# Expert slots of 64, 192, 128 and five of 64 rows, weight pieces split by 2048 columns, and a join by an identity product

## The chip, the cores and the metric

The kernel runs on one core of one Trainium2 chip, as one launch. The metric is device microseconds of that launch. Engines are named as the profile names them: PE (matrix products), DVE (vector), ACT (activation), POOL, and SP, whose queue issues the weight transfers.

## The reference

Two transformer-like blocks run one after the other on 256 tokens of width 1024. The first has two layers (attention with convolution, then a recurrent mixer) with two feed-forward nets each; the second has a mixer and a dense feed-forward net, then a mixer and a mixture of eight experts. The change is about the last stage, the experts, whose weights are some 277 MB of float32:

```python
def _moe(h, w_router, w_gate, w_up, w_down):
    logits = (h @ w_router).astype(jnp.float32)
    top_val, top_idx = lax.top_k(logits, TOP_K)          # TOP_K = 2
    top_w = jax.nn.softmax(top_val, axis=-1)
    gates = jnp.sum(jax.nn.one_hot(top_idx, N_EXPERTS, dtype=jnp.float32) * top_w[..., None], axis=-2)
    out = jnp.zeros_like(h)
    for e in range(N_EXPERTS):
        out = out + gates[..., e:e + 1] * _swiglu_2(h, w_gate[e], w_up[e], w_down[e])
    return out
# _swiglu_2(h, g, u, d) = (silu(h @ g) * (h @ u)) @ d;  h is 256 x 1024, g and u 1024 x 2816, d 2816 x 1024
```

With the reference's own inputs the router gives the eight experts 60, 49, 129, 90, 47, 57, 26 and 54 tokens.

## The kernel before

**Pieces and splits.** Every weight matrix is read in pieces of 1 MB (128 partitions x 2048 columns of float32) into a pool of four buffers, `raw`, by DMAs that SP issues (`load`, L300). An expert has 33 pieces: per chunk of 512 of the 2816 inner columns two for gate, two for up and two for down (the sixth chunk has 256 columns and half as many). `split` turns a piece into a high part and a low part, which PE takes in its fast float32 format: ACT copies with rounding (`wh`, recorded on the helper's line L222) and DVE subtracts the copy from the piece (`wl`, L231). It does so in halves of 1024 columns, each half in one of eight buffers of `wh` and of `wl`; in some of the earlier nets one or two further slots are added (`ext`). A raw buffer is free, and SP issues the next piece into it, when DVE has read it.

**Slots.** The tokens of an expert are gathered into a slot of fixed size. Expert 0 has slot 0; the others are put by size into slots 1 to 7. A slot of 128 rows has its tokens split in two operands, high and low, and takes three products per weight row of 128 (high with high, low with high, high with low; `mm3`, L334 to L337). A slot of 64 rows ("half") puts high and low side by side into one operand of 128 columns and takes two (`prod`, L429): rows 0 to 63 of the result hold the high part and rows 64 to 127 the low part, and these have to be added. Before, slots 0, 2, 3 and 4 hold 128 rows, slots 5, 6 and 7 hold 64, and slot 1, the largest expert, holds 128 + 64 rows ("big"), of which the second part works as a half. A count that doesn't fit is caught by a flag at the end, which runs all experts again in a loop for the rest.

**Order.** The slots run one after the other as `order = [0, 5, 2, 6, 3, 7, 4]`; the six chunks of the big slot are hung into them by the table `plan` (which run of the order and after which chunk). While one slot runs, the tables, gathered operands and gates of the next one are made in between (`tick`, `make`). The first chunk of expert 0 is computed for all 256 tokens ahead of the routing, and its rows are gathered afterwards (`head`). A scheduler then sets the order of all instructions on each engine from this program and the buffers.

**Joining.** For a half, `glu` joins high and low rows of the gate and of the up result: ACT copies rows 64 to 127 out of PSUM, DVE adds them to rows 0 to 63, ACT takes the Silu from SBUF, and DVE multiplies. `glu_T` then turns the result by PE transposes and splits it again for the down product. For a full slot ACT takes the Silu straight from PSUM and DVE multiplies with the other bank.

Of the kernel before, what the change touches and what calls it, by code (L numbers as in the profile page):

```python
# [8 lines left out]
F32 = mybir.dt.float32  # L9
# [183 lines left out]
class K:  # L193
    def __init__(self, ctx, tc, A, out, dbg=None):
# [3 lines left out]
        self.h_p = e(tc.tile_pool(name="wh", bufs=8))  # L198
        self.l_p = e(tc.tile_pool(name="wl", bufs=8))
# [106 lines left out]
    def split(self, raw, nk, n, pin=False):  # L306

        out = []
        per = max(1, 1024 // n)
        for k0 in range(0, nk, per):  # L310
            m = min(per, nk - k0) * n
            if self.ext and self.turn >= 8:
                hl = self.slot(self.ext[self.turn - 8], [128, 2, 1024], F32R)
                h, l = hl[:, 0], hl[:, 1]
            else:
                h = self.h_p.tile([128, 1024], F32R, tag="wh", name="wh")
                l = self.l_p.tile([128, 1024], F32R, tag="wl", name="wl")
            self.turn = (self.turn + 1) % (8 + len(self.ext))
            r = raw[:, k0 * n:k0 * n + m]
# [6 lines left out]
            out.append([(h[:, i * n:(i + 1) * n], l[:, i * n:(i + 1) * n]) for i in range(m // n)])  # L326
# [1067 lines left out]
    def moe(self, h, res, xT, defer):  # L1394
# [3 lines left out]
        lg = self.lg  # L1398

# [96 lines left out]
        def make(got, i, m, half, pcol, gcol):  # L1496
# [5 lines left out]
            eT = self.slot(i % 2, [128, 8, 128] if half else [128, 2, 8, 128], F32R)  # L1502
# [7 lines left out]
        first = make(got, 0, mt[:, 0:512], False, [pos[:, t, 0:1] for t in range(2)], None)  # L1510
# [45 lines left out]
        self.tt(over, cs[:, 0:1], cs[:, 2:3], OP.max)  # L1556
        self.stt(over, cs[:, 1:2], -64.0, over, OP.add, OP.max)
        self.stt(over, cs[:, 5:6], 64.0, over, OP.add, OP.max)
# [7 lines left out]
        self.ts(room, place, 1.0, 2.0, OP.is_equal, OP.add)  # L1566
        self.ts(place, place, 4.5, op0=OP.is_gt)
        self.tt(place, room, place, OP.subtract)
# [14 lines left out]
        def expert(src, got, out, **kw):  # L1583
# [7 lines left out]

            self.ffn(src, 0, got["xk"], [0], fin, half=got["half"], **kw)
# [279 lines left out]
```

## Time and profile before

| | |
|---|---|
| time, 3 runs | median 2261.82 us (2258.93 to 2261.97) |
| the profiled execution's own time | 2259.85 us |
| its span, first to last instruction | 2258.0 us |
| mean granted TensorE clock | 0.996 |
| busy, whole span | PE 97%, PE weight load 80%, DVE 76%, ACT 59%, POOL 4% |
| weight DMAs of the experts | 264 of 1 MB |

The shares are over the whole span, in which the stages differ. From about 1440 us on the experts run, and the table says little of them: the prediction reads that stretch by itself. PE's busy time counts matmuls whose ends overlap, so 97% does not mean that PE could do no more.

### The profile page before, as it was taken

What the parts mean: (1) busy time and instruction counts of PE and PEld (TensorE: products, weight loads), DVE (VectorE), ACT (ScalarE), POOL (GpSimd) and SP (SyncE); (2) the same over time, 40 slices, a digit from 0 to 9 for tenths busy, and PEclk for the clock granted to TensorE, in tenths of its full rate; (3) what the DMA queues carried; (4) which work ended last, traced back from release to release, by engine and by line L of the source; (5) the groups of instructions that cost most, each with busy time, mean ns of one, the idle gap of its engine ahead of it and who ended that gap; (6) DMA issues with size and microseconds to landing.
All of it is one profiled execution on the core that took longest, in us unless ns stands there. A gap on an engine that the chain in (4) does not pass through costs nothing.

```text
span 2258.0 us, 29602 instructions
## 1 busy us (share of the span) xinstructions
PE 2200.2 (97%) x10976; PEld 1812.7 (80%) x10976; DVE 1719.0 (76%) x2205; ACT 1336.0 (59%) x1819; POOL 92.9 (4%) x152
## 2 busy tenths in 40 slices
PE   8999999999999999999999999999999999999998
PEld 6888878888888788887888878887788777877777
DVE  6785967658657886675755666889888999889997
ACT  6445554445436744456544475677767776767764
POOL 0001000000000100030000111000000000000000
PEclk9999999999999999999999999999999999999999
DMA  8784258758764587533555442689988888989886
GB/s 339 267 317 163 99 191 318 258 194 311 262 222 159 193 318 264 207 130 131 215 186 183 143 160 108 249 338 336 336 331 326 326 335 320 344 329 347 325 328 242
DMA packets 82263, 572.92 MB, mean 254 GB/s; under 512 B 9373, under 2 KB 9685, under 8 KB 15424
## 3 DMA queue, kind: packets, MB, share of 16 engines
q1 hardware_dynamic: 77616, 556.73, 66.5%
q0 software_dynamic: 3920, 13.12, 1.7%
q8 instruction: 88, 1.44, 0.2%
q10 hardware_dynamic: 576, 1.11, 0.1%
q14 instruction: 63, 0.52, 0.1%
HBM read 569.80 MB, written 1.12 MB: 253 GB/s over the span
## 4 chain that ended last, share of the span: by engine, by line
PE 46%; DVE 5%; ACT 3%; issue 2%; DMA 1%; POOL 1%; ACTq 0%; DVEq 0%; POOLq 0%
PE mm L334 7%; PE mm L335 7%; PE mm L337 7%; PE mm L429 5%; PE acc L335 4%; PE acc L334 4%; PE acc L337 4%; DVE wl L231 3%; PE acc L429 2%; ACT wh L222 2%; PE mm L1579 1%; ACT s L222 1%; DVE s L231 1%; PE mm L595 1%; PE mm L1467 1%
## 5 line engine op out<-in xcount | busy, mean ns | idle before, releaser
L231 DVE TENSOR_TENSOR wl<-raw,wh 128x1024 fp32r<-128x1024 f32 (+1 forms) x908 | 1078.5, 1216 | 272.4 <-ACT wh L222 259.4
L222 ACT ACTIVATE wh<-raw 128x1024 fp32r<-128x1024 f32 (+1 forms) x908 | 921.0, 1052 | 371.4 <-PE mm L335 152.7
L334 PE MATMUL mm<-wh,s 128*128 128x512 f32 (+2 forms) x1384 | 515.9, 378 | 3.2 <-ACT s L222 3.2
L335 PE MATMUL mm<-wh,s 128*128 128x512 f32 (+2 forms) x1384 | 511.1, 374 | 1.0 <-DVE s L231 1.0
L222 ACT ACTIVATE s<-mm 128x512 fp32r<-128x512 f32 (+7 forms) x387 | 200.1, 534 | 346.8 <-PE mm L337 88.3
L337 PE MATMUL mm<-wl,s 128*128 128x512 f32 (+2 forms) x1384 | 396.1, 374 | 0.2
L334 PE MATMUL acc<-wh,s 128*128 128x512 f32 x788 | 312.0, 397 | 4.0 <-ACT s L222 2.1
L335 PE MATMUL acc<-wh,s 128*128 128x512 f32 x788 | 310.5, 394 | 2.2 <-DVE s L231 2.2
L334 PEld LDWEIGHTS mm<-wh,s 128*128 128x128 f32 x1384 | 261.2, 189 | 50.6 <-ACT s L222 4.9
L335 PEld LDWEIGHTS mm<-wh,s 128*128 128x128 f32 x1384 | 261.7, 189 | 47.7 <-DVE s L231 3.3
L337 PEld LDWEIGHTS mm<-wl,s 128*128 128x128 f32 x1384 | 249.5, 189 | 46.4 <-DVE wl L231 1.2
L337 PE MATMUL acc<-wl,s 128*128 128x512 f32 x788 | 251.9, 392 | 0.6 <-DVE wl L231 0.5
L334 PEld LDWEIGHTS acc<-wh,s 128*128 128x128 f32 x788 | 148.6, 189 | 35.5 <-ACT s L222 3.2
L335 PEld LDWEIGHTS acc<-wh,s 128*128 128x128 f32 x788 | 149.0, 189 | 32.4 <-DVE s L231 4.0
L337 PEld LDWEIGHTS acc<-wl,s 128*128 128x128 f32 x788 | 148.1, 189 | 32.5 <-DVE wl L231 2.2
L429 PE MATMUL mm<-wl,s 128*128 128x512 f32 (+1 forms) x384 | 144.1, 382 | 3.2 <-DVE wl L231 3.1
L429 PE MATMUL mm<-wh,s 128*128 128x512 f32 (+1 forms) x384 | 143.3, 381 | 0.0
L231 DVE TENSOR_TENSOR s<-mm,s 128x512 fp32r<-128x512 f32 (+5 forms) x216 | 128.7, 619 | 17.5 <-ACT s L222 16.7
L987 DVE SCALAR_TENSOR_TENSOR raw<-raw,s 128x1024 f32<-128x1024 f32 x96 | 114.2, 1219 | 4.5 <-DMA raw<-in_ada_w 2.6
L231 DVE TENSOR_TENSOR s<-s,mm 128x512 f32<-128x512 f32 (+1 forms) x93 | 59.6, 641 | 46.7 <-PE mm L337 41.1
L222 ACT ACTIVATE s<-raw 128x1024 fp32r<-128x1024 f32 x50 | 52.5, 1061 | 70.8 <-PE mm L337 33.0
L429 PEld LDWEIGHTS mm<-wl,s 128*128 128x128 f32 x384 | 72.5, 189 | 22.5 <-DVE wl L231 9.2
(308 smaller groups left out, 2187.5 us busy)
## 6 DMA issues: line engine op xcount, KB each, us to landing
raw<-in_moe SPq DMA_DIRECT2D x264, 1024.0 KB, 5.6
raw<-in_f SPq DMA_DIRECT2D x132, 1024.0 KB, 5.9
raw<-in_ada_w SPq DMA_DIRECT2D x48, 1024.0 KB, 5.0
raw<-in_dense SPq DMA_DIRECT2D x33, 1024.0 KB, 4.8
raw<-in_w_in SPq DMA_DIRECT2D x12, 1024.0 KB, 4.9
raw<-in_ow_in SPq DMA_DIRECT2D x8, 1024.0 KB, 5.0
raw<-in_w_out SPq DMA_DIRECT2D x8, 1024.0 KB, 6.2
raw<-in_ew_in SPq DMA_DIRECT2D x7, 1024.0 KB, 5.0
```

What stands on the lines that cost most here:

```text
L222: return self.nc.scalar.activation(out=out, in_=in_, func=func, **kw)
L231: return self.nc.vector.tensor_tensor(out=out, in0=in0, in1=in1, op=op)
L334: mm(out=out, lhsT=xs[i][0], rhs=ws[i][0], start=first and i == 0, stop=False)
L335: mm(out=out, lhsT=xs[i][1], rhs=ws[i][0], start=False, stop=False)
L337: mm(out=out, lhsT=xs[i][0], rhs=ws[i][1], start=False, stop=last and i == n - 1)
L429: self.nc.tensor.matmul(out=out, lhsT=x[0], rhs=w[j][:, c0:c0 + n], start=first and k == 0 and j == 0, stop=last and k == len(ws) - 1 and ...
L595: mm(out=out, lhsT=a, rhs=b, start=j == 0, stop=j == len(todo) - 1)
L987: self.nc.vector.scalar_tensor_tensor(out=src, in0=src, scalar=1.0, in1=self.c_row, op0=OP.mult, op1=OP.mult, accum_out=p[:, 2 * pc + i:2 ...
L1467: mm(out=p[:, k * w:(k + 1) * w], lhsT=h[t][:, a, kk * 128:(kk + 1) * 128], rhs=one[:, o:o + w], start=t == 0, stop=t == 1)
L1579: mm(out=p, lhsT=o[:, t * 128:(t + 1) * 128], rhs=v[:, sl], start=b == 0, stop=b == len(parts) - 1)
```

## The change

It has three parts, all felt mostly in the expert stage.

- **Slots.** Slots 0, 3 and 4 become halves too: the sizes are now 64, 192, 128, 64, 64, 64, 64, 64. The order is `[0, 3, 2, 4, 5, 6, 7]`, and the six chunks of the big slot are hung into runs 1, 3, 4, 4, 5 and 6. The flag's limits follow the sizes. By the counts above every expert fits (60 in slot 0; 129, 90, 57, 54, 49, 47, 26 in slots 1 to 7), so the loop behind the flag does not run.
- **Splits.** The buffers of `wh` and `wl` are four of 2048 columns instead of eight of 1024; two `ext` slots together make a fifth pair, and a single one is no longer used. In the expert stage a piece is copied and subtracted by one instruction each over 2048 columns; elsewhere still by halves of 1024, but both halves share one pair, which is free when both have been used.
- **Join.** For a half, ACT copies rows 64 to 127 of a bank to SBUF as before, but PE adds them to rows 0 to 63 by a product with a 64 x 64 identity that accumulates into the same bank (`self.eye`, `self.low`; the copy goes to the second half of the slot's operand tile). Silu and the multiplication then read PSUM. DVE's two additions are gone.

```diff
-        self.h_p = e(tc.tile_pool(name="wh", bufs=8))
-        self.l_p = e(tc.tile_pool(name="wl", bufs=8))
+        self.h_p = e(tc.tile_pool(name="wh", bufs=4))
+        self.l_p = e(tc.tile_pool(name="wl", bufs=4))
...
     def split(self, raw, nk, n, pin=False):
         out = []
-        per = max(1, 1024 // n)
+        if self.turn < 4:
+            pair = self.h_p.tile([128, 2048], F32R, tag="wh", name="wh"), self.l_p.tile([128, 2048], F32R, tag="wl", name="wl")
+        else:
+            pair = [self.slot(i, [128, 2048], F32R) for i in self.ext]
+        self.turn = (self.turn + 1) % (5 if len(self.ext) == 2 else 4)
+        hi, lo = pair
+        per = nk if self.in_moe else max(1, 1024 // n)
         for k0 in range(0, nk, per):
...
-                self.act(h[:, :m], r, AF.Copy)
+                self.act(hi[:, sl], raw[:, sl], AF.Copy)
...
-            ins = self.tt(l[:, :m], r, h[:, :m].bitcast(F32), OP.subtract)
+            ins = self.tt(lo[:, sl], raw[:, sl], hi[:, sl].bitcast(F32), OP.subtract)
...
     def glu(self, banks, n, g, u, half=False):
         if half:
-            g, u = g[0:64], u[0:64]
-            for v, p in ((g, banks[0]), (u, banks[1])):
+            for j, p in enumerate(banks):
+                v = self.low[0:64, j * 512:j * 512 + n]
                 self.act(v, p[64:128, :n], AF.Copy)
-                self.tt(v, p[0:64, :n], v, OP.add)
-            self.act(g, g, AF.Silu)
-            self.tt(u, u, g, OP.mult)
+                self.nc.tensor.matmul(out=p[0:64, :n], lhsT=self.eye[0:64, 0:64], rhs=v, start=False, stop=True,
+                                      skip_group_check=True)
+            self.act(g[0:64], banks[0][0:64, :n], AF.Silu)
+            self.tt(u[0:64], banks[1][0:64, :n], g[0:64], OP.mult)
             return
...
-        order = [0, 5, 2, 6, 3, 7, 4]
+        order = [0, 3, 2, 4, 5, 6, 7]
 
-        plan = {(6, 1): [(big_end, ())]}
-        for c, (i, at) in enumerate([(1, 4), (3, 0), (3, 3), (5, 0), (5, 3), (2, 2)]):
+        plan = {(6, 2): [(big_end, ())]}
+        for c, (i, at) in enumerate([(1, 4), (3, 1), (4, 0), (4, 4), (5, 3), (6, 0)]):
```

What this moves on the engines is shown at two places. The first is DVE in a run of a half slot beside the full slot's preparation: `wl<-raw,wh` is the split of a piece, `64x512` are the joins and multiplications of the half's chunk, `128x4x64` is the split of its turned result, and `CAST` belongs to the gathering of the next slot. Before (run 1, slot 5):

```order
L231 TENSOR_TENSOR s_227_11373<-mm,s_227_11373 64x512
L231 TENSOR_TENSOR wl<-raw,wh 128x1024 x2
L231 TENSOR_TENSOR s_227_11373<-mm,s_227_11373 64x512
L231 TENSOR_TENSOR wl<-raw,wh 128x1024
L231 TENSOR_TENSOR s_227_11373<-s_227_11373 64x512
L231 TENSOR_TENSOR wl<-raw,wh 128x1024
L231 TENSOR_TENSOR s_232_11634<-mm,s_232_11634 128x4x64
L231 TENSOR_TENSOR wl<-raw,wh 128x1024 x6
```

The same place of the change (run 1, slot 3):

```order
L231 TENSOR_TENSOR wl<-raw,wh 128x2048 x5
L231 TENSOR_TENSOR s_213_10981<-mm,s_213_10981 64x512
L231 TENSOR_TENSOR wl<-raw,wh 128x2048
L231 TENSOR_TENSOR s_218_11244<-mm,s_218_11244 128x4x64
L231 TENSOR_TENSOR wl<-raw,wh 128x2048 x2
L231 TENSOR_TENSOR s_213_10981<-mm,s_213_10981 64x512
```

Per chunk DVE has one instruction of `64x512` instead of three, and one long split per piece instead of two.

The second place is PE at the end of a half's up product (`mm<-wh` and `mm<-wl`), where the down product of the chunk before (`acc`) follows. Before (run 1) the one follows straight on the other:

```order
L429 MATMUL mm<-wh,s_235_11854 128x512
L429 MATMUL mm<-wl,s_235_11854 128x512
L429 MATMUL acc<-wh,s_232_11634 128x512
L429 MATMUL acc<-wl,s_232_11634 128x512
L429 MATMUL acc<-wh,s_232_11634 128x512
```

In the change (run 1) the identity product (L437) that joins the up bank stands one matmul behind the bank's last product:

```order
L428 MATMUL mm<-wh,s_221_11404 128x512
L428 MATMUL mm<-wl,s_221_11404 128x512
L428 MATMUL acc<-wh,s_218_11244 128x512
L437 MATMUL mm<-s_221_11404,rtr 64x512
L428 MATMUL acc<-wl,s_218_11244 128x512
```

PE now has, between the up product and the down product, an instruction that waits for ACT's copy, and the rest of the down product is queued behind it.

## Rows read from the trace of the kernel before

**Rows 1.** The page: busy us and share; tenths busy in 40 slices.

```profile
PE 2200.2 (97%) x10976; PEld 1812.7 (80%) x10976; DVE 1719.0 (76%) x2205; ACT 1336.0 (59%) x1819; POOL 92.9 (4%) x152
...
DVE  6785967658657886675755666889888999889997
...
DMA  8784258758764587533555442689988888989886
```

**Rows 2.** Windows of the expert stage: from:to us, length, busy of each engine, clock, DMA.

```profile
1440.00:2258.00 818.00, 790.86 (x3737) 629.92 (x3735) 730.75 (x778) 588.43 (x694) 0.00 (x0) 0.99 0.87 326
...
1528.00:1646.00 118.00, 113.88 (x542) 88.06 (x540) 109.43 (x121) 95.55 (x119) 0.00 (x0) 0.99 0.91 333
...
1901.00:2002.00 101.00, 99.83 (x484) 82.07 (x483) 85.78 (x85) 70.14 (x81) 0.00 (x0) 1.00 0.90 340
2002.00:2145.00 143.00, 135.12 (x609) 103.27 (x608) 135.00 (x152) 106.45 (x129) 0.00 (x0) 1.00 0.88 330
```

**Rows 3.** Waits of the SP queue, 1450 to 2250 us: total, times, longest.

```profile
SPq L300 <- DVE wl L231: 573.7, 223, 7.1
```

**Rows 4.** Tile raw, 1450 to 2250: duration ns min/median/max, first and last start; landing.

```profile
L231 DVE TENSOR_TENSOR wl<-raw,wh x506: 1202/1218/1227, 1449.2 to 2245.0; 128x1024 fp32r<-128x1024 f32 x169
L222 ACT ACTIVATE wh<-raw x504: 1037/1050/1068, 1449.2 to 2243.3; 128x1024 fp32r<-128x1024 f32 x168
L300 SPq DMA_DIRECT2D raw<-in_moe x249: 327/333/357, 1451.6 to 2233.1; - x125
...
DMA to landing us min/median/max: 4.7/5.7/8.8
```

**Rows 5.** Waits of DVE and ACT, 1450 to 2250 us: total, times, longest.

```profile
DVE wl L231 <- ACT wh L222: 44.3, 61, 2.7
...
ACT wh L222 <- DMA raw<-in_moe: 29.5, 35, 2.0
...
ACT wh L222 <- PE mm L335: 12.6, 27, 2.1
```

**Rows 6.** DVE groups by shape, 1440 to 2258 us: count, busy us, mean ns.

```profile
L231 DVE TENSOR_TENSOR wl<-raw,wh 128x1024 fp32r<-128x1024 f32 x512 | 602.4, 1217 | 49.8 <-ACT wh L222 46.1 <-PE acc L429 0.6
...
L231 DVE TENSOR_TENSOR s<-mm,s 64x512 f32<-64x512 f32 x40 | 27.0, 675 | 2.7 <-ACT s L222 2.7
...
L231 DVE TENSOR_TENSOR s<-s,mm 128x512 f32<-128x512 f32 x24 | 16.5, 686 | 10.5 <-PE mm L337 10.4
L231 DVE TENSOR_TENSOR s<-mm,s 128x512 fp32r<-128x512 f32 x24 | 16.4, 684 | 3.4 <-ACT s L222 3.3
...
L231 DVE TENSOR_TENSOR s<-s 64x512 f32<-64x512 f32 x20 | 13.5, 676 | 0.2
...
L231 DVE TENSOR_TENSOR s<-mm,s 128x256 fp32r<-128x256 f32 x25 | 10.3, 414 | 2.5 <-ACT s L222 2.4
...
L231 DVE TENSOR_TENSOR s<-mm,s 64x256 f32<-64x256 f32 x8 | 3.3, 411 | 0.9 <-ACT s L222 0.9
```

**Rows 7.** ACT groups by shape, 1440 to 2258 us.

```profile
L222 ACT ACTIVATE wh<-raw 128x1024 fp32r<-128x1024 f32 x511 | 509.5, 1051 | 67.0 <-DMA raw<-in_moe 29.5 <-PE mm L335 13.4 <-PE acc L335 9.0
...
L222 ACT ACTIVATE s<-mm 64x512 f32<-64x512 f32 x40 | 23.8, 595 | 31.2 <-PE mm L429 30.7
...
L222 ACT ACTIVATE s<-s 64x512 f32<-64x512 f32 x20 | 12.4, 621 | 1.8 <-DVE s L231 1.8
```

**Rows 8.** Timeline of PE inside a full slot: start us, us.

```profile
1712.28 0.39 PE L334 MATMUL mm<-wh,s 128*128 128x512 f32 x1
...
1713.19 0.39 PE L334 MATMUL mm<-wh,s 128*128 128x512 f32 x1
```

**Rows 9.** Windows with the highest DMA rates, and one with a lower clock.

```profile
15.00:20.00 5.00, 4.90 (x21) 3.73 (x20) 5.00 (x6) 4.67 (x6) 0.00 (x0) 1.00 1.02 412
...
1590.00:1600.00 10.00, 9.52 (x47) 7.10 (x46) 8.59 (x13) 8.05 (x11) 0.00 (x0) 1.00 1.01 404
...
1620.00:1630.00 10.00, 8.36 (x46) 6.85 (x45) 8.94 (x12) 6.84 (x11) 0.00 (x0) 0.83 0.78 265
```

**Rows 10.** Waits of ACT ahead of the experts, 0 to 1430 us.

```profile
ACT wh L222 <- PE mm L335: 138.2, 150, 3.2
```

More of the change, by code (lines that the diff above doesn't have):

```diff
@@ L308, in split @@
         out = []
-        per = max(1, 1024 // n)
-        for k0 in range(0, nk, per):
[L311 to L319, printed above, removed]
+        if self.turn < 4:
[5 more added lines that the diff above has]
+        per = nk if self.in_moe else max(1, 1024 // n)
+        for k0 in range(0, nk, per):
+            m = min(per, nk - k0)
+            sl = slice(k0 * n, (k0 + m) * n)
             with self.tc.issue_after(self.behind.ins) if self.behind else ExitStack():
-                self.act(h[:, :m], r, AF.Copy)
+                self.act(hi[:, sl], raw[:, sl], AF.Copy)
             self.behind = None
-            ins = self.tt(l[:, :m], r, h[:, :m].bitcast(F32), OP.subtract)
+            ins = self.tt(lo[:, sl], raw[:, sl], hi[:, sl].bitcast(F32), OP.subtract)
             if pin:
                 self.pin(ins)
-            out.append([(h[:, i * n:(i + 1) * n], l[:, i * n:(i + 1) * n]) for i in range(m // n)])
+            out.append([tuple(v[:, k * n:(k + 1) * n] for v in pair) for k in range(k0, k0 + m)])
         return out
@@ L1398, in moe @@
         lg = self.lg
+        self.eye = self.small("rtr", 128, F32R, bufs=1)
+        nc.vector.tensor_copy(out=self.eye, in_=self.ident)
         up0 = [self.piece(A["moe"][0], j * 128 * 2048, 4, 512) for j in range(4)]
@@ L1501, in make @@
             yield
-            eT = self.slot(i % 2, [128, 8, 128] if half else [128, 2, 8, 128], F32R)
+            eT = self.slot(i % 2, [128, 2, 8, 128], F32R)
+            if half:
+                got["low"] = eT[:, 1].rearrange("p k n -> p (k n)")
+                eT = eT[:, 0]
             got.update(xk=operand(eT, half), half=half, o32=oneT.bitcast(F32))
@@ L1509, in moe @@
         got = {}
-        first = make(got, 0, mt[:, 0:512], False, [pos[:, t, 0:1] for t in range(2)], None)
+        first = make(got, 0, mt[:, 0:512], True, [pos[:, t, 0:1] for t in range(2)], None)
         for _ in range(5):
@@ L1555, in moe @@
         over = self.small("over", 1, bufs=1)
-        self.tt(over, cs[:, 0:1], cs[:, 2:3], OP.max)
+        self.tt(over, cs[:, 0:1], cs[:, 3:4], OP.max)
+        self.stt(over, over, 64.0, cs[:, 2:3], OP.add, OP.max)
         self.stt(over, cs[:, 1:2], -64.0, over, OP.add, OP.max)
-        self.stt(over, cs[:, 5:6], 64.0, over, OP.add, OP.max)
         over_i = self.small("overi", 1, I32, bufs=1)
@@ L1565, in moe @@
         room = self.small("room", 8, bufs=1)
-        self.ts(room, place, 1.0, 2.0, OP.is_equal, OP.add)
-        self.ts(place, place, 4.5, op0=OP.is_gt)
-        self.tt(place, room, place, OP.subtract)
+        self.ts(room, place, 1.0, 2.0, OP.is_equal, OP.mult)
+        self.ts(place, place, 2.0, 1.0, OP.is_equal, OP.add)
+        self.tt(place, room, place, OP.add)
         self.ts(place, place, 64.0)
@@ L1590, in fin @@
                     self.stt(ye[:, sl], acc[hh], got["gs"], g2[:, sl], OP.mult, OP.mult)
+            self.low = got.get("low")
             self.ffn(src, 0, got["xk"], [0], fin, half=got["half"], **kw)
@@ L1703, in moe @@
                 m = (i + 1) % 2 * 512
-                todo.append(make(after, i + 1, mt[:, m:m + 512], n > 4, [posS[t][:, n:n + 1] for t in range(2)],
+                todo.append(make(after, i + 1, mt[:, m:m + 512], n != 2, [posS[t][:, n:n + 1] for t in range(2)],
                                  lambda n=n: [gateS[t][:, n:n + 1] for t in range(2)]))
```

10 lines of the change are left out of this document (6 added, 4 removed).

## The prediction

> **What bounds the kernel now.** I read the page first, to find the stretch that the change is about. DVE and the DMA engines are moderately busy up to about 1440 us and near full from there on, where the experts run [rows 1]. In the windows of that stretch, 818 us long, three things are near their limit at once: DVE is busy 730.75 us (89%), the DMA engines 87% at 326 GB/s, and PE shows 790.86 us, which is too much, since its matmuls overlap [rows 2]. So I read PE by the spacing of matmuls: four of 512 columns take 1713.19 - 1712.28 = 0.91 us, 0.2275 us each [rows 8]. A piece of a full slot is 12 of them (2.73 us), of a half 8 (1.82 us), of the big slot 20 (4.55 us).
>
> Then the waits, to see which of the three ends last. The SP queue stands 573.7 of 800 us waiting for DVE's subtraction `wl`: the next weight DMA goes out when DVE has freed a raw buffer [rows 3]. DVE in turn waits little (44.3 us for ACT's copy), and ACT waits 29.5 us for DMAs and 12.6 us for PE to free a buffer [rows 5]. In runs of a half slot DVE is 93% and 94% busy (109.43 of 118, 135.00 of 143), in the run of the full slot 3 it is 85% (85.78 of 101) and PE sets the pace [rows 2]. So DVE is the limit in half runs, PE in full runs, and a ring of four raw buffers ties them together.
>
> The ring can be counted. Its 249 DMAs start between 1451.6 and 2233.1 us, 781.5 / 248 = 3.151 us apart [rows 4]. Four buffers make a turn of 12.6 us for one: 5.7 us from issue to landing, 1.05 us for ACT's first half, 2 x 1.218 = 2.44 us for DVE's two halves (the second copy lies beside the first subtraction) [rows 4]. That leaves 3.4 us in which a landed piece waits for an engine that is at other work. This turn is what the change has to shorten.
>
> **The change part by part.**
>
> *Long splits.* Two instructions become one. DVE needs 676 ns for 512 columns from SBUF and 1217 for 1024 [rows 6], so 135 ns are fixed, and 2048 columns should take 2.30 us instead of 2.43: 0.135 us x 256 pieces = 35 us less of DVE. ACT has 621 and 1051 ns [rows 7], 191 ns fixed: 1.91 instead of 2.10 us, 49 us less. Against that stands latency: DVE now starts after the whole copy, so a piece's own work in the ring rises from 3.49 to 1.91 + 2.30 = 4.21 us.
>
> *Join.* The additions of DVE go: 27.0 + 3.3 us [rows 6], with the busy time of the 512 and 256 column forms. The multiplication of a half reads PSUM instead of SBUF, at 675 against 676 ns, so it costs what it did. PE gets 82 identity products (68 of 512 columns, 14 of 256): 75 x 0.2275 = 17 us.
>
> *Three slots become halves.* PE does one product less on 132 weight rows of 512 columns for three experts, less 16 for the first chunk of expert 0, which is done for all tokens: 380 x 0.2275 = 86 us less. On DVE three experts exchange one multiplication per chunk for another (686 against 675 ns, nothing), and 15 splits of the turned result over 512 columns for 15 over 256: 15 x (684 - 414) = 4 us less. ACT gets 28 more copies of 595 ns and 6 short ones, some 19 us; its net is about 30 us less.
>
> So DVE loses 35 + 30 + 4 = 69 us, and PE 86 - 17 = 69 us. DVE's work per piece was 602.4 / 256 = 2.35 us of splitting and (730.75 - 602.4) / 256 = 0.50 us of other work, 2.85 in all; it becomes 2.85 - 69 / 256 = 2.58 us.
>
> *What of it the ring lets through.* The period is (5.7 + 4.21 + w) / 4, with w the time in which a landed piece waits. Bounds: if DVE stays as busy as in 1440 to 2258, 2.58 / 0.893 = 2.89 us, then w = 1.6 us; if waits stay at 3.4 us the period is 3.33 us. I take w by what a landed piece finds: ACT, busy some 70% of the time (588.43 of 818 [rows 2]), has on average half of a 1.91 us copy left (0.7 us), and DVE, near 90%, half of a 2.30 us subtraction (1.0 us); together 1.7, and 0.1 for the few waits on PE, 1.8 us. The waits were longer mainly because DVE was behind, which it is less now. This gives (5.7 + 4.21 + 1.8) / 4 = 2.93 us, and 2.58 / 2.93 = 88% for DVE. Over the 253 pieces of the steady stretch (half of the 506 splits [rows 4]): 253 x (3.151 - 2.93) = 56 us less.
>
> A period of 2.93 us is 358 GB/s. The trace had 404 GB/s over 10 us among the experts and 412 over 5 us at the start, with the DMA engines' share at 1.0 [rows 9], which is 2.6 us for a piece; so I don't count the DMA engines as the limit. The Trainium skill (DMA: Bandwidth & Descriptors, Specifications) gives about 358 GB/s as the HBM limit for a core; by it no more than my 56 us could come, and the sum would stay 2206. The windows above it speak against that limit for a core that runs alone.
>
> *The identity products on PE.* Each stands one to some sixteen matmuls behind the product that it joins, and what is queued behind it is the down product, whose result only the end of the slot needs, or the next up product. The wait is at least nothing, where a piece is late anyway, and at most a copy that ACT has begun plus its own, 1.91 + 0.60 = 2.5 us. In a half run the PE work is 1.82 us per piece with about 0.3 of transposes, gathering and identity products; two waits of 2.5 us in six pieces add 0.8 us: 2.9 us, still not above the period. I cost it at nothing, and DVE's pace is the cover.
>
> *The big slot.* Six pieces take PE 27 us and the ring 18. PE falls 9 us behind, two pieces; four buffer pairs hold that, just. All its chunks now lie in half runs, where PE gains 0.8 us per piece, so they don't add up.
>
> *Ahead of the experts* pairs are freed whole. There ACT waits for PE to free `wh` (138.2 us in 150 waits [rows 10]), so splits run ahead of PE, and half a piece less lead is hidden. Nothing, with bounds of 3 us less (a luckier order) and 6 us more (transitions, when DVE is at the norms); I add 2.
>
> Sum, against the profiled execution's own 2259.85 us (within 2 us of the median 2261.82): 2259.85 - 56 + 2 = **2206 us**.
>
> **The rivals.**
>
> *The ring stays slow (same or a little faster).* If the long instructions make pieces miss each other more, w is 2.2 to 2.7 us and the period 3.03 to 3.15: 2230 to 2262 us. For it: landing was as long as 8.8 us at times [rows 4]. Against: both engines get less to do.
>
> *Latency of whole pieces (slower).* Place: between landing and the free raw buffer. It takes 0.72 us more of own work there; should waits stay at 3.4 us, the period is 3.33 us and the time 2259.85 + 253 x 0.18 = 2305 us. It decides from w = 12.6 - 5.7 - 4.21 = 2.7 us on. For it: there are four raw buffers still, and SP already waits for them most of the time [rows 3]. Against: DVE at 93% in half runs shows that most of w was its own queue.
>
> *DVE sets the pace alone (much faster).* At the 94% of a half run, 2.58 / 0.94 = 2.74 us: 104 us less, 2156 us. It needs w = 1.1 us.
>
> *PE's clock.* A window with PE busy 8.36 of 10 us had a granted clock of 0.83 [rows 9], so part of it at the lower of the two levels, 1.2 GHz. Halves leave PE idle more. If the mean falls to 0.8, half pieces need (1.82 + 0.3) / 0.8 = 2.65 us, below the period; only the big slot's 4.55 us grow to 5.7, 33 x 1.15 = 38 us, if nothing hides them: 2244 us. The Trainium skill (TensorE: Matmul & The Clock Gate, part 1) says that the lower clock is the default and that idling brings it back; the window agrees.
>
> That the loop behind the flag runs is excluded by the counts.
>
> **How the numbers follow.** Forecast (2170 to 2230): 0.58. Slow ring 0.18, of which a third ends within 0.2%. Latency, slower: 0.13. DVE alone: 0.06. Clock 0.05. The range, 2165 to 2264, reaches from w = 1.2 to the point where the gain is gone; with half of "DVE alone" and most of "latency" outside it leaves out some 0.2. Faster by over 0.2% (4.5 us, about what a measurement of this kernel can tell): 0.58 + 0.12 + 0.06 + 0.04 = 0.80; within 0.06; slower 0.14.
>
> **What would show it.** Splits of 2.30 us on DVE and 1.91 on ACT; 256 periods near 2.93 us; DVE's share among the experts at 88% with some 660 us busy, SP still waiting for `wl`. Wrong would be: a period above 3.1 with DVE below 83% (latency), PE waits at the identity line of more than 0.5 us on average in the big slot's chunks, a granted clock below 0.95, or a start of the experts that moves by more than 6 us.

## The result, and the profile after

The change makes the kernel slower. Four runs give a median of 2283.34 us (2281.99 to 2285.68), against 2261.89 us for the kernel before in the same comparison; the ratio is 1.0098, with a 95% interval of 1.0081 to 1.0116. That is 21 us more. The forecast was 2206 us, 77 us lower; the time lies outside the range of 2165 to 2264. The profiled execution took 2283.6 us with a span of 2281.8 us and a granted clock of 0.991.

The page of the kernel after, its busy times and the rows of DVE and of the DMA engines over 40 slices, answers to [rows 1]:

```profile
PE 2174.7 (95%) x10654; PEld 1752.4 (77%) x10654; DVE 1661.9 (73%) x1900; ACT 1303.8 (57%) x1589; POOL 100.3 (4%) x152
...
DVE  5785967657657876665745666888788788887887
...
DMA  8684248758755587533655432789898888889886
```

PE, DVE and ACT have less to do, as forecast, and the kernel is longer: DVE lost 57 us over the whole span and now shows 7s and 8s among the experts where it had 8s and 9s. The window that [rows 2] had, 1440 to 2258 us, says the same of the stage by itself:

```profile
1440.00:2258.00 818.00, 751.27 (x3376) 561.29 (x3376) 674.38 (x498) 567.47 (x466) 0.64 (x1) 0.99 0.87 325
```

DVE is at 82% and PE at 92%, both lower than before, the granted clock shows the same 0.99, and the weights come at 325 instead of 326 GB/s. So no engine became the bound; something waits. The tile `raw` from 1450 to 2250 us shows the ring (count, duration ns min/median/max, first and last start), beside [rows 4]:

```profile
L231 DVE TENSOR_TENSOR wl<-raw,wh x249: 2272/2286/2295, 1449.4 to 2248.3; 128x2048 fp32r<-128x2048 f32 x125
L222 ACT ACTIVATE wh<-raw x248: 1888/1907/1925, 1449.0 to 2246.3; 128x2048 fp32r<-128x2048 f32 x124
L300 SPq DMA_DIRECT2D raw<-in_moe x248: 327/333/356, 1451.7 to 2248.2; - x124
...
DMA to landing us min/median/max: 4.6/5.8/8.1
```

The period is (2248.2 - 1451.7) / 247 = 3.225 us, against 3.151 before and 2.93 in the forecast. Four periods are 12.9 us; less 5.8 for landing, 1.91 for the copy and 2.29 for the subtraction, 2.9 us of waiting are left. The forecast had 1.8.

The waits of the same stretch (total us, times, longest) show who waits; they answer to [rows 3] and [rows 5]:

```profile
SPq L300 <- DVE wl L231: 551.6, 213, 7.6
...
ACT s L222 <- PE mm L428: 111.9, 62, 4.8
DVE wl L231 <- ACT wh L222: 99.0, 87, 5.9
ACT wh L222 <- PE acc L428: 25.3, 12, 5.3
ACT wh L222 <- DMA raw<-in_moe: 24.5, 31, 2.2
...
PE mm L437 <- ACT s L222: 8.9, 21, 0.5
```

ACT now stands 111.9 us in 62 waits at the copies `s` that join a half, waiting for PE to end the gate or up product (L428). The same wait in the same stretch of the kernel before (L429 there):

```profile
ACT s L222 <- PE mm L429: 42.9, 29, 3.9
```

There are 82 such copies now and 48 before, so each waits 1.4 us on average instead of 0.9. DVE's wait for ACT's copy of a piece grew from 44.3 to 99.0 us. The identity products (L437) themselves make PE's matmuls wait only 8.9 us. So the chain to be tested is: PE ends a bank later, ACT stands at its join, the next piece's copy stands behind that, DVE behind the copy, SP behind DVE.

The groups of DVE, ACT and PE by shape over the whole stage, 1440 to 2282 us, beside [rows 6] and [rows 7]:

```profile
L231 DVE TENSOR_TENSOR wl<-raw,wh 128x2048 fp32r<-128x2048 f32 x257 | 582.7, 2287 | 104.8 <-ACT wh L222 103.0
...
L222 ACT ACTIVATE wh<-raw 128x2048 fp32r<-128x2048 f32 x256 | 482.8, 1908 | 68.0 <-PE acc L428 25.3 <-DMA raw<-in_moe 24.5 <-PE mm L428 12.6
...
L222 ACT ACTIVATE s<-mm 64x512 fp32r<-64x512 f32 x68 | 40.4, 594 | 97.5 <-PE mm L428 96.8
...
L437 PE MATMUL mm<-s,rtr 64*64 64x512 f32 x68 | 29.6, 441 | 7.5 <-ACT s L222 7.4
```

The long instructions take what was forecast (2287 and 1908 ns), but save less: DVE's splits fell from 602.4 to 582.7 us, 20 us and not 35.

### The profile page after: what moved, and what is told of

It is laid out like the page before. It is cut to its first block, busy times and chain, and to the rows that moved or that the text cites. A ratio compares the mean times of both kernels' runs of the same rounds, so it can differ in the third digit from the quotient of the medians.

```text
span 2281.8 us, 28012 instructions
## 1 busy us (share of the span) xinstructions
PE 2174.7 (95%) x10654; PEld 1752.4 (77%) x10654; DVE 1661.9 (73%) x1900; ACT 1303.8 (57%) x1589; POOL 100.3 (4%) x152
## 4 chain that ended last, share of the span: by engine, by line
PE 39%; DVE 9%; ACT 6%; issue 2%; DMA 1%; POOL 1%; ACTq 0%; DVEq 0%; POOLq 0%
PE mm L428 8%; DVE wl L231 7%; ACT wh L222 5%; PE mm L333 4%; PE mm L334 4%; PE mm L336 4%; PE acc L428 3%; PE acc L334 3%; PE acc L333 3%; PE acc L336 2%; DMA raw<-in_moe 1%; PE mm L1470 1%; ACT s L222 1%; PE mm L596 1%; PE mm L1585 1%
## 5 line engine op out<-in xcount | busy, mean ns | idle before, releaser
L231 DVE TENSOR_TENSOR wl<-raw,wh 128x1024 fp32r<-128x1024 f32 (+3 forms) x658 | 1065.9, 1644 | 356.5 <-ACT wh L222 354.5
L222 ACT ACTIVATE wh<-raw 128x1024 fp32r<-128x1024 f32 (+3 forms) x658 | 897.1, 1393 | 451.5 <-PE mm L334 196.0
L333 PE MATMUL mm<-wh,s 128*128 128x512 f32 (+2 forms) x1144 | 428.5, 380 | 1.6 <-ACT s L222 1.3
L334 PE MATMUL mm<-wh,s 128*128 128x512 f32 (+2 forms) x1144 | 425.3, 376 | 1.5 <-DVE s L231 1.5
L222 ACT ACTIVATE s<-mm 128x512 fp32r<-128x512 f32 (+10 forms) x445 | 225.5, 523 | 346.3 <-PE mm L428 117.0
L336 PE MATMUL mm<-wl,s 128*128 128x512 f32 (+2 forms) x1144 | 322.2, 376 | 1.9 <-DVE wl L231 1.9
L428 PE MATMUL mm<-wl,s 128*128 128x512 f32 (+1 forms) x656 | 248.6, 386 | 32.6 <-DVE wl L231 32.2
L333 PE MATMUL acc<-wh,s 128*128 128x512 f32 x680 | 270.1, 398 | 4.7 <-DVE s L231 2.8
L334 PE MATMUL acc<-wh,s 128*128 128x512 f32 x680 | 268.4, 395 | 0.8 <-DVE s L231 0.8
L428 PE MATMUL mm<-wh,s 128*128 128x512 f32 (+1 forms) x656 | 244.1, 380 | 0.0
L336 PE MATMUL acc<-wl,s 128*128 128x512 f32 x680 | 213.8, 393 | 0.0
L428 PEld LDWEIGHTS mm<-wl,s 128*128 128x128 f32 x656 | 124.0, 189 | 73.4 <-DVE wl L231 51.0
L333 PEld LDWEIGHTS acc<-wh,s 128*128 128x128 f32 x680 | 128.6, 190 | 32.9 <-ACT s L222 4.2
L334 PEld LDWEIGHTS acc<-wh,s 128*128 128x128 f32 x680 | 129.2, 190 | 27.1 <-DVE s L231 1.7
L428 PEld LDWEIGHTS mm<-wh,s 128*128 128x128 f32 x656 | 124.3, 189 | 24.2 <-issue 3.8
L428 PE MATMUL acc<-wl,s 128*128 128x512 f32 x308 | 125.4, 411 | 16.6 <-DVE wl L231 16.6
L428 PE MATMUL acc<-wh,s 128*128 128x512 f32 x308 | 125.8, 411 | 2.1 <-ACT wh L222 2.1
```

The costliest lines, as they stand in the source:

```text
L222: return self.nc.scalar.activation(out=out, in_=in_, func=func, **kw)
L231: return self.nc.vector.tensor_tensor(out=out, in0=in0, in1=in1, op=op)
L333: mm(out=out, lhsT=xs[i][0], rhs=ws[i][0], start=first and i == 0, stop=False)
L334: mm(out=out, lhsT=xs[i][1], rhs=ws[i][0], start=False, stop=False)
L336: mm(out=out, lhsT=xs[i][0], rhs=ws[i][1], start=False, stop=last and i == n - 1)
L428: self.nc.tensor.matmul(out=out, lhsT=x[0], rhs=w[j][:, c0:c0 + n], start=first and k == 0 and j == 0, stop=last and k == len(ws) - 1 and ...
```

## The experiments

Two theories stood at the start of the second series. **Theory A**, the rival "latency of whole pieces": a piece's own work in the ring, 4.2 instead of 3.5 us, keeps a raw buffer bound for longer. **Theory B**: PE gets a piece later and in one lump, so it ends a bank later, and ACT, in order, stands at the join. All ratios are to the kernel before in the same comparison. For two kernels of different comparisons I subtract ratios; 0.1% is 2.26 us.

### Which part of the change costs

The four kernels undo parts of it; the code below shows only the lines that matter. The first takes back the splits and buffers, the second the join, the third both, the fourth the slots and the join:

```diff
-        self.h_p = e(tc.tile_pool(name="wh", bufs=4))
-        self.l_p = e(tc.tile_pool(name="wl", bufs=4))
+        self.h_p = e(tc.tile_pool(name="wh", bufs=8))
+        self.l_p = e(tc.tile_pool(name="wl", bufs=8))
...
+                h = self.h_p.tile([128, 1024], F32R, tag="wh", name="wh")
+                l = self.l_p.tile([128, 1024], F32R, tag="wl", name="wl")
```

```diff
...
-                self.nc.tensor.matmul(out=p[0:64, :n], lhsT=self.eye[0:64, 0:64], rhs=v, start=False, stop=True,
-                                      skip_group_check=True)
...
+                self.tt(v, p[0:64, :n], v, OP.add)
...
```

```diff
...
-        order = [0, 3, 2, 4, 5, 6, 7]
+        order = [0, 5, 2, 6, 3, 7, 4]
...
```

New slots and PE join, short splits. 

> New slots and the join on PE, but the splits of before (halves of 1024 columns, eight buffers each). Theory latency (the long splits lengthen a piece's stay in the four raw buffers by 0.7 us and delay ACT and DVE behind them): faster than before, 2215 to 2245 us, DMA issues of the experts 3.0 to 3.1 us apart. Theory join (ACT stands at its copies and PE at the identity products, 112 us of ACT waiting for the half product): 2270 to 2285 us, as the change. Theory slots (half slots and their order themselves make PE wait for pieces and ACT for PE): 2265 us or more.

Measured 2245.44 us, ratio 0.9935 (0.9921 to 0.9949).

New slots and long splits, DVE join. 

> New slots and the long splits, but the join by DVE's additions as before. Theory latency: still slow, 2275 to 2300 us. Theory join: at or below before, 2230 to 2260 us. Theory slots: 2275 us or more.

Measured 2275.25 us, 1.0062 (1.0046 to 1.0078).

New slots alone. 

> New slots alone: splits and join as before. Theory latency: 2225 to 2255 us (86 us of products gone from PE, 14 more additions pairs, some 17 us, on DVE). Theory join: 2220 to 2250 us. Theory slots: 2265 us or more.

Measured 2244.73 us, 0.9936 (0.9920 to 0.9951).

Long splits with buffer pairs alone. 

> Long splits and their buffer pairs alone: slots, order and join as before. Theory latency: slower than before by 15 us or more, 2277 to 2300 us, issues 3.2 us apart or more. Theory join: 2245 to 2262 us. Theory slots: 2245 to 2262 us.

Measured 2271.98 us, 1.0055 (1.0040 to 1.0071).

So the slots gain 0.64% (14 us). The join makes no difference that can be told where splits are short (0.9935 against 0.9936) and costs 0.36% (8 us) on top of long ones (1.0098 against 1.0062). The long splits with their pairs cost 1.26% (28 us) on the new slots, 0.55% (12 us) on the old ones. The splits turn a gain into a loss.

### What of the long splits costs

Each of these starts from the new slots with DVE's join and the change's buffer pairs. The first keeps all instructions short; the second and third make only ACT's copy or only DVE's subtraction long (`pieces` runs an instruction in steps of so many columns):

```diff
-        per = nk if self.in_moe else max(1, 1024 // n)
+        per = max(1, 1024 // n)
```

```diff
-            ins = self.tt(lo[:, sl], raw[:, sl], hi[:, sl].bitcast(F32), OP.subtract)
+            ins = self.pieces(sl, 1024, lambda c: self.tt(lo[:, c], raw[:, c], hi[:, c].bitcast(F32), OP.subtract))
```

```diff
-                self.act(hi[:, sl], raw[:, sl], AF.Copy)
+                self.pieces(sl, 1024, lambda c: self.act(hi[:, c], raw[:, c], AF.Copy))
```

> The half slots alone (2244.7 us), but with the change's four buffer pairs of 2048 columns for wh and wl, each freed as a whole; all copies and subtractions still over 1024 columns. Theory (latency: a raw buffer is bound for longer because DVE starts only after a whole copy): the instructions are short, so nothing but the later start of the experts is added: 2245 to 2251 us, period of the weight DMAs 3.08 us. Rival (the pairs: ACT waits for PE to free a pair that is freed as a whole): 2265 to 2280 us, ACT's waits of wh for PE above 40 us.

Measured 2249.17 us, 0.9952 (0.9938 to 0.9965): the pairs by themselves cost 0.16% (4 us), with overlapping intervals.

> The half slots alone, with buffer pairs, in the experts one copy of 2048 columns on ACT and two subtractions of 1024 on DVE. Theory (latency): the piece's own work is 1.91 + 2.44 = 4.35 us instead of 3.49, so as slow as with both long (2275 us) or slower: 2272 to 2290 us, period 3.20 to 3.25. Rival (DVE's long instruction is what holds up its other work): 2245 to 2255 us. Rival (the long copy on ACT holds up ACT's other work): as the theory, and then the next kernel is fast.

Measured 2263.21 us, 1.0012 (1.0002 to 1.0022).

> The half slots alone, with buffer pairs, in the experts two copies of 1024 columns on ACT and one subtraction of 2048 on DVE. Theory (latency): own work 2.10 + 2.29 = 4.39 us, 2272 to 2290 us, period 3.20 to 3.25. Rival (the long copy on ACT is the harm): 2245 to 2255 us. Rival (the long subtraction on DVE is the harm): as the theory, and the kernel before this one is fast.

Measured 2267.49 us, 1.0037 (1.0021 to 1.0052). Either long instruction costs over half of what both do, 14 and 19 us of 25. Theory A had both mixed kernels as slow as the fully long one or slower, since their own work is longest; that failed.

Then the ring itself, one buffer less with short splits (from the third kernel of the first series):

```diff
-        self.raw_p = e(tc.tile_pool(name="raw", bufs=4))
+        self.raw_p = e(tc.tile_pool(name="raw", bufs=3))
```

> The half slots alone, short splits, with three raw buffers instead of four in the whole kernel. Theory (latency through the ring of raw buffers): three buffers share a turn of at least 5.7 + 3.49 + 1.0 = 10.2 us, so the period is 3.4 to 3.7 us and the time 2325 to 2400 us. Rival (DVE's and PE's work sets the pace, the ring only follows): at most 2265 us, DVE's busy share in the experts stays above 88%.

Measured 2285.99 us, 1.0108 (1.0090 to 1.0126): far less than theory A forecast. The tile `raw`, 1450 to 2250 us, of the new slots alone and then with three buffers:

```profile
L300 SPq DMA_DIRECT2D raw<-in_moe x249: 327/333/356, 1452.4 to 2215.8; - x125
...
DMA to landing us min/median/max: 4.7/6.4/8.8
```

```profile
L300 SPq DMA_DIRECT2D raw<-in_moe x244: 327/333/353, 1451.7 to 2246.3; - x122
...
DMA to landing us min/median/max: 4.6/4.9/7.7
```

With four buffers the period is 763.4 / 248 = 3.078 us, a turn of 12.3 us; with three it is 794.6 / 243 = 3.270 us, a turn of 9.8 us. The turn lost 2.5 us and the period grew by 0.19: landing gave 1.5 us (6.4 to 4.9) and the waits 1.0. The wait in the ring is therefore no fixed quantity that adds to the own work, but mostly slack that shrinks when it is needed. By this measure the 0.7 us of own work that long splits add would cost about 0.7 / 2.5 x 0.19 x 253 = 13 us, an estimate that takes the slack as even.

### Late hand-over to PE

The short-split kernel with pairs again, but PE takes the second half of each piece first. Nothing is longer; PE only starts when all of a piece is split, as with long splits (full slots are turned round likewise, by lines not shown):

```diff
+    def second_half_first(self, v):
+        h = len(v) // 2
+        return v[h:] + v[:h] if self.in_moe else v
...
-        for k, (x, w) in enumerate(zip(xs, ws)):
+        for k, (x, w) in enumerate(self.second_half_first(list(zip(xs, ws)))):
...
```

> The half slots with buffer pairs and short splits (2249.2 us), but in the experts PE takes the second half of each piece first, so that it starts on a piece only when all of it is split. Work and instructions are the same, and so is the time that a raw buffer is bound by its own piece. Theory A (own work in the ring of raw buffers is what the long splits cost): 2246 to 2253 us. Theory B (long splits hand a piece to PE later and in one lump, so the last product of a bank ends later, and ACT, which takes instructions in order, stands longer at the copy that joins a half): 2258 to 2275 us, and ACT's waits of s for PE's half products go from 60.7 us to 80 or more.

Measured 2266.91 us, 1.0022 (1.0012 to 1.0032): 0.70% (16 us) slower than 0.9952, with the same instructions on every engine. The waits from 1450 to 2240 us, of the kernel without and then with the reversal (where L437 is the line of the half products):

```profile
ACT s L222 <- PE mm L428: 60.7, 50, 4.0
...
DVE wl L231 <- ACT wh L222: 34.7, 41, 2.6
PE mm L428 <- DVE wl L231: 20.5, 48, 0.8
...
PE acc L428 <- DVE wl L231: 14.1, 33, 0.8
...
DVE s L231 <- ACT s L222: 4.8, 9, 1.4
```

```profile
ACT s L222 <- PE mm L437: 79.6, 49, 4.6
...
PE mm L437 <- DVE wl L231: 34.4, 60, 1.7
...
DVE wl L231 <- ACT wh L222: 27.0, 44, 3.2
PE acc L437 <- DVE wl L231: 25.3, 31, 1.6
DVE s L231 <- ACT s L222: 17.3, 34, 1.4
```

ACT's waits at the joins grew by 19 us, to the 80 that theory B had, next to 16 us lost. Theory A had at most 2253 us. PE waits 59.7 instead of 34.6 us for the low parts. One link of the chain does not show here: DVE's waits for the copies of pieces did not grow (34.7 to 27.0 us); those of its other work (`s`, the additions of the joins among it) for ACT did (4.8 to 17.3 us). The granted clock fell too: it is 0.994 to 0.996 in the runs without the reversal and 0.988 to 0.995 in those with it. So the 16 us may hold a share of PE at its lower clock; the part on why the prediction was wrong estimates such shares.

### The joins without their wait

Both kernels of the next pair let the join, Silu and multiplication read rows that lie ready in SBUF. The use of the gate and up results is left out; every product and split is made. Short splits first, then long:

```diff
     def glu(self, banks, n, g, u, half=False):
+        if self.in_moe:
+            banks = self.x
         if half:
```

> The half slots with buffer pairs and short splits (2249.2 us); in the experts the join, Silu and multiplication read the residual rows from SBUF instead of PE's two banks, so neither ACT nor DVE waits there for the up product. This leaves out the use of the gate and up results; every product, split and instruction stays. Both theories: a little faster, 2230 to 2249 us. It is the base for the next kernel.

Measured 2245.86 us, 0.9924 (0.9912 to 0.9937).

> The half slots with buffer pairs and long splits (2275.2 us), with the join, Silu and multiplication of the experts reading the residual rows instead of PE's banks, as in the kernel before this one. Theory A (own work in the ring): the long splits still cost what they did, 26 us, here 20 to 30 us more than the kernel before this one. Theory B (ACT's wait for PE at the join): what they cost falls below 10 us.

Measured 2249.15 us, 0.9946 (0.9932 to 0.9960). Between them lies 0.22% (5 us), with overlapping intervals, where the same step cost 1.10% (25 us) with the wait (0.9952 to 1.0062). ACT's and DVE's largest waits, 1450 to 2240 us, with long splits and the joins' wait, and then without it:

```profile
ACT s L222 <- PE mm L428: 83.7, 47, 4.5
DVE wl L231 <- ACT wh L222: 62.2, 82, 3.3
...
ACT wh L222 <- DMA raw<-in_moe: 37.7, 42, 3.0
```

```profile
ACT wh L222 <- DMA raw<-in_moe: 61.2, 63, 2.9
...
DVE wl L231 <- ACT wh L222: 50.2, 63, 2.4
```

ACT, no longer held at the joins, now waits for the weights first: it is early where it was late. Some four fifths of the cost of the long splits on the new slots go when nothing waits for PE at the joins. By which path those waits cost time is argued, not shown. That the next copies stand behind the joins is in the order of the instructions; the Trainium skill (PSUM — Partial Sum Buffer, Engine vs sequencer instructions) says of ScalarE's and VectorE's queues that they are strictly first in, first out. The rows of the change fit that: ACT's 111.9 us at the joins come with 99.0 us in which DVE waits for copies. In the reversed order, as said, DVE's waits grew at its other work instead. The granted clock moves along: 0.987 to 0.991 with long splits and the joins' wait, 0.992 to 0.995 without it.

The same edit on the change itself, with its identity products kept:

> The change; in the experts the join's copies, Silu and multiplication read the residual rows from SBUF instead of PE's banks (the use of the gate and up results is left out; every instruction stays, the identity products too). Theory B (ACT's waits for PE at the joins are what the change loses by): it falls by 35 us or more, to 2215 to 2248 us, and without those waits the change is faster than before, since DVE has less to do. Theory A (own work in the ring): 2272 us or more.

Measured 2254.51 us, 0.9969 (0.9957 to 0.9980): 1.29% (29 us) less than the change. The direction fits theory B; the size does not quite (35 us or more, to at most 2248, was expected), and with all waits at the joins gone the PE join is not faster than DVE's (0.9969 against 0.9946), though DVE has less to do.

### More raw buffers from a shared pool

```diff
-        self.raw_p = e(tc.tile_pool(name="raw", bufs=4))
+        self.raw_p = e(tc.tile_pool(name="raw", bufs=8))
...
-            pair = self.h_p.tile([128, 2048], F32R, tag="wh", name="wh"), self.l_p.tile([128, 2048], F32R, tag="wl", name="wl")
+            pair = self.h_p.tile([128, 2048], F32R, tag="wh", name="wh"), self.raw_p.tile([128, 2048], F32R, tag="raw", name="wl")
```

> The change, but raw and wl take their buffers of 2048 columns from one pool of eight instead of four and four, so that a piece can be fetched ahead while wl buffers are free. Theory A (the ring of four raw buffers is what limits): at most 2268 us. Theory B: 2274 to 2290 us, little changed, since the transfers are not what the engines wait for; a loss is possible, because wl then waits for raw.

Measured 2964.26 us, 1.3098 (1.3079 to 1.3116). It tells nothing of the two theories: the shared pool binds the whole kernel, not the experts alone. The waits of SP's queue over the whole span:

```profile
SPq L299 <- DVE wl L230: 1543.6, 337, 26.6
SPq L299 <- PE mm L335: 339.7, 51, 15.0
SPq L299 <- PE acc L335: 252.3, 36, 32.4
```

A raw buffer now follows a `wl` buffer, so a load waits until PE has used a low part: 592 us on two rows, where the longest such row of SP's queue is 19.0 us in the whole span of the kernel before and of the change.

### Joins placed later

The join is written after the down product of the chunk before, and ACT's copies for it are held behind the copy of that product's second piece:

```diff
-                if c == 5 or 0 < c and not (not self.in_moe):
+                if c == 5:
                     trans_chunk(c)
...
                 w = down_w(c - 1)
+                copied = self.copied
...
-                if (not self.in_moe):
-                    trans_chunk(c)
+                if self.in_moe:
+                    with self.tc.issue_after(copied.ins):
+                        join(c, banks)
+                trans_chunk(c)
```

On the change: 

> The change, its result kept, with the joins of the experts written after the down product of the chunk before, and ACT's copies for them held behind the copy of that product's second piece, so that ACT comes to them when PE is done; the big slot's joins stay where they are. Theory B: ACT's waits of s for PE's half products fall below 60 us (110.0 before) and the time to 2250 to 2272 us. Theory A: 2278 to 2290 us.

Measured 2296.58 us, 1.0155 (1.0142 to 1.0168), slower still and outside what either theory had. Waits, 1450 to 2240 us:

```profile
PEld mm L451 <- DVE s L231: 60.7, 26, 5.3
ACT wh L222 <- PE mm L428: 54.4, 29, 4.9
PE mm L451 <- DVE s L231: 49.8, 23, 4.9
...
ACT s L222 <- PE mm L428: 28.7, 16, 4.2
```

The wait at the joins did fall, from 110.0 us in that stretch to 28.7. But the transposes (L451) now come to PE before DVE has made what they turn, PE stands there 49.8 us, and ACT waits 54.4 us for PE to free `wh`. The wait was moved, not removed, and the granted clock was lower still (0.979 to 0.981).

On long splits with DVE's join: 

> The half slots with long splits and DVE's join (2275.2 us), with the joins placed as in the kernel before this one. Theory B: 2245 to 2266 us. Theory A: 2270 to 2280 us. Rival of both (DVE's additions, placed late, hold up DVE's splits): slower than 2280 us.

Measured 2260.18 us, 0.9994 (0.9983 to 1.0006): 0.68% (15 us) of the 25 us came back, as theory B had it.

On the new slots with short splits: 

> The half slots alone with short splits (2244.7 us), with the joins placed as in the two kernels before this one. Theory B: ACT's waits are small with short splits already, so a little faster at most: 2232 to 2246 us. Slower than 2250 us would say that late joins cost elsewhere.

Measured 2252.38 us, 0.9960 (0.9947 to 0.9973): 0.24% (5 us) slower, with intervals that overlap. Late joins gained only where the wait at the joins is long and the join is DVE's.

### What sets the pace when the joins don't

Both start from the short-split kernel with pairs (0.9952). The first leaves out DVE's subtraction for the second half of each piece, and PE takes the first half's low part twice; the second loads half of each piece and splits it twice:

```diff
-            ins = self.tt(lo[:, sl], raw[:, sl], hi[:, sl].bitcast(F32), OP.subtract)
+            if not (self.in_moe and k0):
+                ins = self.tt(lo[:, sl], raw[:, sl], hi[:, sl].bitcast(F32), OP.subtract)
```

```diff
     def load(self, src, off, n):
+        n = n // 2 if self.in_moe else n
```

> The half slots with buffer pairs and short splits (2249.2 us); in the experts DVE subtracts only for the first half of a piece, and PE takes that low part for both halves. This leaves out the low parts of the second halves, some 250 subtractions of 1.2 us, 300 us of DVE's work. If DVE's work sets the pace of the experts where splits are short, the period falls to 2.8 us or less and the time to 2180 us or less. If it does not (transfers, or PE with its waits), 2222 to 2246 us.

Measured 2218.80 us, 0.9820 (0.9802 to 0.9837).

> The half slots with buffer pairs and short splits (2249.2 us); in the experts each weight DMA brings only half of its piece (512 KB), and both halves are split from it. This leaves out half of the weights; all splits and products stay. If the transfers set the pace or a good part of it, 2215 us or less; if DVE's work does, 2232 to 2250 us.

Measured 2227.38 us, 0.9855 (0.9837 to 0.9873). 287 us less of DVE's subtractions (599.6 to 312.5 in the stage) give 1.32% (30 us), half the bytes 0.97% (22 us): neither sets the pace alone. Windows over the same 12 and 12 pieces tell why (they begin and end where weights are issued, so PE's matmuls in them differ a little). The first stretch is mostly half products, in the second there are products of the big slot, a chunk of 256 columns and the gathering of the next operand; first the kernel with pairs, then the one with half of the subtractions:

```profile
1938.40:1971.90 33.50, 30.13 (x109) 19.66 (x109) 31.55 (x31) 24.88 (x29) 0.00 (x0) 0.95 0.98 365
1971.90:2016.50 44.60, 43.10 (x202) 33.57 (x200) 39.09 (x46) 31.78 (x39) 0.00 (x0) 1.00 0.82 302
```

```profile
1920.50:1950.70 30.20, 26.48 (x105) 18.55 (x106) 19.23 (x19) 26.81 (x31) 0.00 (x0) 1.00 0.97 371
1950.70:1992.90 42.20, 41.16 (x192) 32.16 (x191) 25.21 (x32) 29.54 (x37) 0.00 (x0) 1.00 0.91 334
```

In the second stretch PE is busy 97% and 98% of the time whatever DVE has to do. In the first DVE goes from 94% to 64% and the stretch loses only 3.3 us, with the DMA engines' share at 0.98 and 0.97 in both; the clock, 0.95 and then 1.00, may have a part in the 3.3 us. Freed from DVE, this half stretch meets the transfers, and the other meets PE.

## Why the prediction was wrong

**The step that failed is "What of it the ring lets through".** It put w at 1.8 us, as half an instruction of ACT and of DVE. It was 2.9 us, so the period rose to 3.225 instead of falling to 2.93, and the 56 us did not come. Two things were wrong in it. It counted "0.1 for the few waits on PE", read from [rows 5], where no wait at a join is shown: [rows 7] has 30.7 us of them before the copies of 512 columns, the trace of before 42.9 us in 29 waits, and they were not weighed. And it took these waits as unchanged by splits that hand a piece to PE later; they became 111.9 us. From 1450 us on they are 51.2 us with the new slots alone, 60.7 with the pairs, 83.7 with long splits as well and 110.0 in the change, so the splits are not the whole of the growth. The rule for w could have been tried on the kernel before: ACT busy some 70% with copies of 1.05 us and DVE near 90% with subtractions of 1.22 give 0.4 + 0.5 + 0.1 = 1.0 us, where the count from [rows 4] leaves 3.4. The rule misses most of the waiting there already. The reversed order shows that late hand-over alone costs 16 us, and the kernels without the joins' wait that some 20 of the 25 us that the long splits cost on the new slots go with that wait.

**One period for all 253 pieces** was the second fault of that step. Some stretches are PE's, as the part on what bounds the kernel said of full runs, and there DVE's relief gives little; the sum left it out. With a half of DVE's splitting gone, far more than the 69 us of the change, only 30 us came.

**Sizes.** *Long splits*: 20 us less on DVE and 27 on ACT (509.5 to 482.8) instead of 35 and 49. Subtractions that follow each other overlap: 512 of 1217 ns would be 623 us, and [rows 6] has 602.4 busy. *Three slots become halves* was right in direction: 14 us by itself, the only gain of the three parts. *Join*: nothing with short splits, though on the new slots it takes 52 us of additions from DVE (46.0 + 5.8 in the trace of the new slots alone, 68 of 512 columns and 14 of 256); 8 us of loss with long ones. The waits at the *identity products* were costed at nothing on PE, and PE's matmuls do wait only 8.9 us there. With long splits the join on PE comes with more waiting of ACT at the joins (83.7 to 110.0 us) and of DVE for copies (62.2 to 96.9, all from 1450 to 2240 us); why is open. *Ahead of the experts*: the first expert piece is issued at 1346.4 instead of 1341.2 us, 5 us, within the bounds of -3 and +6.

**The clock.** The granted clock stayed above the 0.95 that the prediction set as a sign, but it fell, and the sum had no term for that: 0.988 to 0.991 in the runs of the change, where the kernel before has 0.993 to 0.998. The runs of one kernel go with it: eighteen of the kernel before, taken together, reach from 2255.62 us at 0.998 to 2264.82 us at 0.993, 1.8 us for 0.001. By that, as an estimate, up to 9 of the change's 21 us go with the lower clock (medians 0.996 and 0.991), up to 11 of the 16 us of the reversed order (0.996 and 0.990), and up to 14 of the 25 us of the long splits (0.996 and 0.988). The windows from 1800 to 1900 us of the kernel before and of the change show it (0.98 and 0.95), with PE busy 94.90 and 88.48 us:

```profile
1800.00:1900.00 100.00, 94.90 (x439) 74.75 (x438) 92.25 (x102) 73.18 (x90) 0.00 (x0) 0.98 0.88 327
```

```profile
1800.00:1900.00 100.00, 88.48 (x382) 64.98 (x381) 81.02 (x60) 67.77 (x57) 0.00 (x0) 0.95 0.85 312
```

One such fall in the change, in windows of 2 us: PE stands for more than half of 4 us, and then runs for some 6 us at the lower of its two levels, 1.2 GHz, with 7 matmuls in a window where it has 10 at full clock:

```profile
1816.00:1818.00 2.00, 0.80 (x8) 0.42 (x5) 1.14 (x1) 1.98 (x4) 0.00 (x0) 1.00 0.89 274
1818.00:1820.00 2.00, 0.70 (x3) 0.39 (x4) 2.00 (x3) 2.00 (x3) 0.00 (x0) 0.85 0.61 254
...
1822.00:1824.00 2.00, 2.00 (x7) 1.52 (x6) 1.56 (x1) 0.71 (x1) 0.00 (x0) 0.50 0.67 279
...
1828.00:1830.00 2.00, 2.00 (x10) 1.67 (x9) 1.91 (x3) 1.91 (x1) 0.00 (x0) 1.00 0.00 0
```

The reversal lowered the clock with the same instructions on every engine, so there the late hand-over came first and the clock after it. How the loss parts between the lower clock and the waits by themselves was not tested.

**The rivals.** "Latency of whole pieces" named the right outcome, and w ended beyond its point of 2.7 us; its sign, a period above 3.1 us with DVE below 83%, came too (3.225 us, 82%). Its mechanism, own work added to a fixed wait, did not hold: three buffers cost 39 us and not the 80 or more that it gives, and the mixed kernels lay between instead of at the top. By the three buffers own work would bear some 13 us of the loss; the kernels without the joins' wait leave 5. "DVE alone" fell with the halved subtractions. "PE's clock" asked for a mean of 0.8, which did not come; its direction did.

**What stays open.** On the old slots the long splits cost 12 us though the waits at half joins were smaller (28.5 us) than before; some 4 us may be the pairs ahead of the experts (first piece at 1345.2 instead of 1341.2 us) and another 4 to 5 the granted clock (0.992 to 0.994), by the estimate above; the rest was not taken apart. So the joins' wait is shown as the cause of the long splits' cost only for the new slots. All these kernels are ordered anew by the scheduler, so a few us of each difference may be its choice.

The fastest kernel with the whole computation is the new slots alone, with or without the PE join: 0.9936 and 0.9935, 14 us faster than the kernel before and 37 us faster than the change.

## What to carry to other kernels

Where one long instruction takes the place of two short ones, look past its own duration to the consumer that could start on the first half, and to every in-order engine that waits for that consumer: most of the loss here went with ACT's waits at copies that the edit doesn't touch. A wait that is suspected can be priced by letting its instruction read ready data in two kernels that differ in the disputed edit; the difference of the differences is its price, with all that moves along, here the clock. And a stage whose bound alternates is summed stretch by stretch, since relief of one engine counts only where that engine is last.

## What the runs showed of the hardware

- Two subtractions of 1024 columns take 602.4 / 256 = 2.35 us of DVE's busy time and one of 2048 takes 2.29: joining them saves 0.06 us, not the 0.135 us that single durations suggest.
- The time to landing is no constant: 6.4 us in the median for 1 MB at a period of 3.08 us, 4.9 us with one buffer less at 3.27 us, and for 512 KB 3.2 us, as the tile `raw` of the kernel with half the bytes shows (1450 to 2200 us):

```profile
DMA to landing us min/median/max: 3.0/3.2/5.4
```

- The weights came at 371 GB/s over 30 us. The Trainium skill (DMA: Bandwidth & Descriptors, Specifications) has about 358 GB/s as the HBM limit of a core; the measurement decides, and for this core running alone that figure is no limit.
